# A two-layer encoder trunk: its opening rewritten, three projections first and memory's units behind

## The chip, the cores and the metric

One core of a Trainium2 chip runs the whole kernel as one program. The engines are TensorE (PE, with its weight loads as PEld), VectorE (DVE), ScalarE (ACT), GpSimd (POOL) and SyncE (SP, which here only issues DMAs). Each engine works through its own list of instructions in a fixed order; semaphores make one wait for another. The metric is the device time in microseconds (us) of one execution, less is better.

## The reference, cut to what matters

Batch 1, 1024 tokens, width 1024, two layers (A, then B). All tensors are float32.

```
mem_n = rmsnorm(mem, norm_mem)                       # 256 memory tokens
for i in range(2):
    h = rmsnorm(x, norm_mix[i])                      # x * rsqrt(mean(x^2)) * gain
    mk, mv = split(mem_n @ w_mem_kv[i])              # 4 heads of 64 each
    q, k, v, qm = split(h @ w_in[i])                 # A: 12 q, 4 k, 4 v heads; B: 12 of each; 4 qm heads
    y_tok = windowed_gqa(q, k, v, sink)              # i = 0; neighbourhood_attn for i = 1
    y_mem = softmax(qm mk^T / 8) mv
    x = x + concat(y_tok, y_mem) @ w_out[i]
    h = rmsnorm(x, norm_ffn[i])
    x = x + (silu(h @ w_gate) * (h @ w_up)) @ w_down[i]
out = rmsnorm(x, norm_final)
```

The norm of a token is one factor r = rsqrt(mean(x^2) + eps) for all its features. So (x * gain * r) @ W is the same as ((x * gain) @ W) * r: the factor can be multiplied in before the projection or behind it.

## The kernel before, in words

Tokens lie along the free dimension, in two halves of 512; features lie on the 128 partitions, in eight blocks k = 0..7. A weight is kept as units of 128 output columns: a tile of 128 x 1024, eight blocks of 128 x 128.

Every product is done in three passes. An operand is split into a high part (a cast to fp32r, on ACT, `hi`, L106) and a low part (operand minus high part, on DVE or POOL, `lo`, L109). `steps` (from L133) issues for each k three matmuls: high by high, high by low, low by high. A unit on one half is 24 matmuls of 512 columns; a unit on the 256 memory tokens is 24 of 256 columns.

The opening is everything ahead of layer A's attention:

- Memory's units: eight (four of each layer) of `w_mem` times `mhl`, the memory tokens times their gain, without the norm's factor. `finish_wm` multiplies the factor in when it reads a sum, and splits the keys (units 0 and 1 of a layer) or transposes and splits the values (units 2 and 3).
- `norms[0]`, the norm of the first half of x: squares on ACT, added up on DVE (`Norm.merge`), summed over partitions by four small matmuls into `st`; DVE adds eps (`nv`), POOL takes the power -0.5 (`nr`), DVE makes a diagonal matrix (`diag`), and a matmul with ones spreads it over all partitions (`bc`). `Norm.split` multiplies x by gain and `bc` and splits the result into `hT`, the operand of the projections.
- `first_dense` then runs three projections of the first half (units 0, 10 and 8 of `w_in_a`: a q and k unit, a memory-query unit, a v unit; their tiles are called wf), and beside them the norm and split of the second half. The sums stay in PSUM.
- `first_units` (in the layer's loop) reads these three sums (`put`), runs the same three units on the second half, transposes v (`vtr`), and fetches the next units (wqq, wqk, ...). From there on the attention's heads run, with the other projections pulled in between; the first scores `S` are those of a memory head, with keys mKH, mKL, which are read back from a buffer in HBM.

Order of work: the program text gives a priority, and a scheduler of the framework that runs at build time lays down the list of each engine, so that the lists don't follow the text in all places. Tiles come from pools with a fixed number of buffers; whoever takes a buffer waits for its last reader. The names in the rows: wm is a memory unit's weight, wf one of the first three units', mm the PSUM tile of a unit's sum, sq a square, mt a memory sum in SBUF, mvT its transpose.

Of the kernel before, what the change touches and what calls it, by code (L numbers as in the profile page):

```python
# [41 lines left out]
def trunk_kernel(ctx: ExitStack, tc: tile.TileContext, a: dict, out: bass.AP):  # L42
# [110 lines left out]
    def first_dense(layer, norm, more=iter(()), split=()):  # L153

        pre = []
        src = a["w_in_a"] if layer == 0 else a["w_in_b"]
        todo = (norm.add(x[k][1]) for k in range(len(norm.xs), NK))
        parts = norm.split(layer, hT[1], 6 if layer else 4)
        for n, u in enumerate(FIRST[layer]):
            w = split[n] if n < len(split) else load_w(src[u], eng=None if layer == 0 else nc.gpsimd, name="wf")  # L160
            if layer:
                wide[:] = True, (4, 2, 3)[n]
            ps = mm_tile()
            for i, _ in enumerate(steps(ps, w, hT[0])):
                next(more, None)
                if layer == 0 and len(norm.xs) < NK:
                    if n or i > 1:
                        run_some(todo, 2)
                elif next(todo, 0) is not None and (n or i > 3):
                    next(parts, None)  # L170
            if n == 1:
                run(more)
            pre.append((w, ps))
        run(parts)
        return pre
# [15 lines left out]
    class Norm:  # L191


        def __init__(self, n=HS, summed=NK):
            self.n, self.acc, self.xs, self.st, self.dg = n, [], {}, None, None
            self.summed = summed
# [90 lines left out]

    with tc.tile_pool(name="mp", bufs=1, reuse_waits="tile") as mp:
        phase[:] = mp, 8, 5
        memt = mp.tile([P, NK, NM], F32, name="memt")  # L290
        warm = mp.tile([P, P], F32, name="warm")
# [3 lines left out]

        def load_wm(i):
            ws[i] = raw_tile("wm")
            nc.sync.dma_start(ws[i], a["w_mem"][i // 4, i % 4])

        def split_wm(i, cs=slice(0, D)):  # L300
            if i not in whl:
                whl[i] = wp.tile([P, 2, D], F32R, tag="whl", name="wm", bufs=3)
            w = whl[i]
            hi(w[:, 0, cs], ws[i][:, cs])
            lo(w[:, 1, cs], ws[i][:, cs], w[:, 0, cs])

        def load_x(f, k):
            t = mp.tile([P, 2, HS], F32, tag=f"x{k}{f}", name=f"x0_{k}{f}")
            nc.sync.dma_start(
                t, a["x"][k : k + 2].rearrange("m p t -> p m t")[:, :, f * HS : (f + 1) * HS]  # L310
            )
            x[k][f], x[k + 1][f] = t[:, 0], t[:, 1]

        ws, whl = {}, {}
        ws[0] = raw_tile("wm0")
        nc.sync.dma_start(memt[:, :2], a["mem"][:, :2])
        nc.scalar.dma_start(ws[0][:, :HS], a["w_mem"][0, 0][:, :HS])
        nc.sync.dma_start(gains, a["gains"])
        nc.sync.dma_start(memt[:, 2:4], a["mem"][:, 2:4])
        nc.scalar.dma_start(ws[0][:, HS:], a["w_mem"][0, 0][:, HS:])  # L320
        nc.sync.dma_start(memt[:, 4:], a["mem"][:, 4:])
        load_wm(1)
        load_x(0, 0)
        load_x(0, 2)
        load_x(0, 4)
        load_x(0, 6)
        load_wm(2)
        nc.sync.dma_start(ident, a["ident"])
        load_wm(3)
        nc.sync.dma_start(sink, a["sink"].to_broadcast([P, NH]))  # L330
        split_wm(0, cs=slice(0, HS))


        mh = []
        mhl = mp.tile([P, NK, 2, NM], F32R, name="mhl")
        mem_norm = Norm(NM)
        for k in range(NK):
            t, g = mhl[:, k], gains[:, 4, k : k + 1]
            nc.scalar.activation(t[:, 0], memt[:, k], AF.Copy, scale=g)
            nc.vector.scalar_tensor_tensor(  # L340
                t[:, 1], memt[:, k], g, t[:, 0].bitcast(F32), op0=ALU.mult, op1=ALU.subtract
            )
            mh.append(t)
            if k == 1:
                split_wm(0, cs=slice(HS, D))
        split_wm(1)
        hT = [[None] * NK, [None] * NK]
        norms = [Norm(), Norm()]
        for k in range(NK):
            norms[0].add(x[k][0])  # L350
        scale = mp.tile([P, NM], F32, name="mscale")
        kept, sums = [], {}

        def finish_wm(i):

            (kh, kl, vm), u, ps = kept[i // 4], i % 4, sums.pop(i)
            t = temp("mt", NM)
            if u < 2:
                nc.vector.tensor_tensor(t, ps[:, :NM], scale, op=ALU.mult)
                hi(kh[:, u], t)  # L360
                lo(kl[:, u], t, kh[:, u])
                return
# [13 lines left out]
        parts, early = iter(()), []  # L376
        for i in range(8):
            if i % 4 == 0:
# [4 lines left out]
                kept.append((kh, kl, vm))  # L383
            if i + 4 < 8:
                load_wm(i + 4)
                load_x(1, 2 * i)
            if i + 2 < 8:
                split_wm(i + 2)
            sums[i] = dense(whl[i], mh, NM)
            if i == 1:  # L390
                for _ in range(2):
                    nc.tensor.matmul(
                        ps_o.tile([P, HS], F32, tag="O", name="warm"), ones, x[6][0], start=True, stop=True
                    )
                norms[0].sums()
                for k in range(NK):
                    mem_norm.add(memt[:, k])
            if i == 2:
                parts = norms[0].split(0, hT[0])
                run_some(parts, 1)  # L400
                mem_norm.sums()
                nc.vector.tensor_scalar(nsink, sink, -1.0, None, op0=ALU.mult)
            if i == 3:
                nc.scalar.copy(scale, mem_norm.scale(ps_t))
                finish_wm(0)
            if i > 3:
                finish_wm(i - 3)
            if i > 2:
                run_some(parts, 2)
            if i > 5:  # L410
                early.append(load_w(a["w_in_a"][FIRST[0][i - 6]], name="wf"))

        def last_units():
            for i in (5, 6, 7):
                yield
                yield
                yield
                finish_wm(i)

        pre = first_dense(0, norms[1], last_units(), early)  # L420
        for l, (kh, kl, vm) in enumerate(kept):
            nc.sync.dma_start(memk_d[l, 0], kh.rearrange("p m k -> p (m k)").bitcast(F32))
            nc.sync.dma_start(memk_d[l, 1], kl.rearrange("p m k -> p (m k)").bitcast(F32))
            nc.sync.dma_start(memv_d[l], vm.rearrange("p b m i d -> p (b m i d)").bitcast(F32))

    for layer in range(2):
        is_a = layer == 0
        with tc.tile_pool(name=f"ap{layer}", bufs=1, reuse_waits="tile") as ap:
# [59 lines left out]
            class Unit:  # L488
# [371 lines left out]

        with (
# [725 lines left out]
```

## Time and profile before

| what | value |
|---|---|
| median of 3 runs | 2135.73 us (2135.31 to 2136.31) |
| profiled execution, first to last instruction (span) | 2130.8 us |
| lies around the span | 4.9 us (the median less the span) |
| PE busy | 2097.1 us, 98% |
| DVE, ACT, POOL busy | 1517.2 us (71%), 1065.8 us (50%), 576.8 us (27%) |

Sections 1 and 2 of the profile's page give the busy share of each engine over the whole span and in 40 slices; the first slice and a half (53 us a slice) hold the opening. PE's digit is 8 in the first slice and 9 in all the others but the last. The chain that ended last is 90% PE. How to read the rows further down: the timeline gives start, length, engine, line, operation and tiles of instructions that follow one another on an engine (xN: N of them merged), and in brackets how long the engine stood idle before them and whom it waited for.

### The profile page before, as it was taken

Reading aid. Unit: us, or ns where it says so; the run is one execution under the profiler, and the core shown is the slowest. Engines: PE = TensorE matmul, PEld = TensorE weight load, DVE = VectorE, ACT = ScalarE, POOL = GpSimd, SP = SyncE. Lnnn points to the kernel's source line nnn. Section 1 sums busy time; section 2 is a strip of 40 time slices with the busy share of each in tenths; the row PEclk is TensorE's granted clock in tenths of the full one; section 3 lists DMA queues with packets and bytes.
Section 4 is the critical chain, followed back from the end, with each engine's and each line's share of the span. In section 5 each row is a group of like instructions: output and inputs, shape, how many; then the busy total and the mean of one; then the engine's idle time right before and its main releaser. Section 6 shows DMA issues by size and latency. Waiting matters only on the chain.

```text
span 2130.8 us, 29089 instructions
## 1 busy us (share of the span) xinstructions
PE 2097.1 (98%) x10320; PEld 1752.8 (82%) x10320; DVE 1517.2 (71%) x2481; ACT 1065.8 (50%) x2046; POOL 576.8 (27%) x618
## 2 busy tenths in 40 slices
PE   8999999999999999999999999999999999999998
PEld 7788888878888888888778888888888888888887
DVE  7677787788666666867766666667976666677676
ACT  6577775443434334344465666654443434344442
POOL 0343330233443430000233223203243443410000
PEclk9999999999999999999999999999999999999999
DMA  6321028323323327866232222275233323267662
GB/s 247 114 92 44 31 68 295 112 90 123 109 90 111 105 106 252 307 210 210 70 92 82 73 62 68 87 254 165 64 113 112 109 95 114 100 246 258 199 226 89
DMA packets 121042, 287.29 MB, mean 135 GB/s; under 512 B 12224, under 2 KB 20672, under 8 KB 120896
## 3 DMA queue, kind: packets, MB, share of 16 engines
q1 hardware_dynamic: 113584, 272.71, 38.1%
q10 hardware_dynamic: 7312, 12.72, 1.6%
q8 instruction: 82, 1.34, 0.3%
q14 instruction: 64, 0.52, 0.1%
HBM read 210.40 MB, written 68.94 MB: 131 GB/s over the span
## 4 chain that ended last, share of the span: by engine, by line
PE 90%; DVE 3%; ACT 3%; DMA 1%; issue 1%; POOL 1%; SPq 0%; DVEq 0%; ACTq 0%; POOLq 0%
PE X L952 17%; PE Y L952 16%; PE mm L139 16%; PE X L1383 11%; PE Y L1383 8%; PE po L139 8%; PE S L619 3%; PE O L682 3%; PE pT L662 3%; PE X L1034 2%; PE Y L1034 2%; DMA wd_kept<-in_w_dn 1%; POOL wS L909 0%; DMA x<-in_x 0%; PE bc L255 0%
## 5 line engine op out<-in xcount | busy, mean ns | idle before, releaser
L952 PE MATMUL Y<-hB,wgu 128*128 128x512 f32 x1056 | 255.5, 391 | 0.8 <-ACT c L972 0.8
L952 PE MATMUL X<-hB,wgu 128*128 128x512 f32 x1056 | 254.8, 391 | 0.0
L1383 PE MATMUL X<-hB,wd 128*128 128x512 f32 (+1 forms) x1092 | 243.8, 383 | 1.0 <-DVE x L1347 1.0
L109 DVE TENSOR_TENSOR wgu<-wS,wgu 128x1024 fp32r<-128x1024 f32 (+1 forms) x124 | 152.9, 1233 | 121.8 <-ACT wgu L106 121.5
L1383 PEld LDWEIGHTS X<-hB,wd 128*128 128x128 f32 x1092 | 200.1, 188 | 42.0 <-issue 2.4
L952 PEld LDWEIGHTS Y<-hB,wgu 128*128 128x128 f32 x1056 | 196.7, 188 | 43.4 <-ACT c L972 1.7
L952 PEld LDWEIGHTS X<-hB,wgu 128*128 128x128 f32 x1056 | 195.9, 188 | 39.9
L647 POOL TENSOR_SCALAR p<-p,stat 128x384 f32<-128x384 f32 (+1 forms) x256 | 139.7, 565 | 310.8 <-DVE stat L644 207.5
L139 PE MATMUL mm<-hT,wqk 128*128 128x512 f32 x672 | 196.1, 405 | 1.5 <-DVE KL L109 1.5
L106 ACT CAST wgu<-wS 128x1024 fp32r<-128x1024 f32 (+1 forms) x124 | 114.3, 923 | 149.6 <-POOL wS L909 124.6
L139 PE MATMUL po<-yT,wo 128*128 128x512 f32 x768 | 184.8, 394 | 0.0
L1383 PE MATMUL Y<-hB,wd 128*128 128x512 f32 x792 | 180.7, 389 | 0.1
L1383 PEld LDWEIGHTS Y<-hB,wd 128*128 128x128 f32 x792 | 148.5, 188 | 31.6 <-ACT hB L106 0.5
L240 POOL TENSOR_TENSOR nr<-nv,neg_half 128x4 f32<-128x4 f32 (+1 forms) x12 | 11.3, 938 | 600.5 <-DVE nv L239 600.5
L139 PEld LDWEIGHTS po<-yT,wo 128*128 128x128 f32 x768 | 142.8, 188 | 29.7 <-issue 1.0
L952 PE MATMUL X<-hT,wgu 128*128 128x512 f32 x624 | 150.2, 391 | 0.0
L106 ACT CAST hB<-b_raw 128x512 fp32r<-128x512 f32 x154 | 89.5, 618 | 110.6 <-DMA b_raw<-b_d 95.0
L909 POOL TENSOR_TENSOR wS<-wgu_raw 128x512 f32<-128x512 f32 x44 | 61.1, 1388 | 294.8 <-DVE wgu L109 294.8
L952 PEld LDWEIGHTS X<-hT,wgu 128*128 128x128 f32 x624 | 116.8, 188 | 26.3
L634 ACT ACTIVATE p<-p,stat 128x256 f32<-128x256 f32 (+1 forms) x192 | 112.4, 587 | 51.5 <-DVE stat L630 49.2
L109 DVE TENSOR_TENSOR pl<-pT,ph 128x384 fp32r<-128x384 f32 (+1 forms) x256 | 118.0, 493 | 19.4 <-ACT ph L106 16.5
L952 PE MATMUL Y<-hT,wgu 128*128 128x512 f32 x528 | 129.9, 390 | 0.0
(185 smaller groups left out, 4201.5 us busy)
## 6 DMA issues: line engine op xcount, KB each, us to landing
wgu_raw<-in_w_gu SPq DMA_DIRECT2D x92, 512.0 KB
wd_raw<-in_w_dn SPq DMA_DIRECT2D x70, 512.0 KB
b_raw<-b_d SPq DMA_DIRECT2D x70, 512.0 KB
b_d<-c SPq DMA_DIRECT2D x88, 256.0 KB
b_d<-t SPq DMA_DIRECT2D x66, 256.0 KB
wo_raw<-in_w_out SPq DMA_DIRECT2D x32, 512.0 KB
xr_d<-x ACTq DMA_DIRECT2D x32, 256.0 KB
xr<-xr_d SPq DMA_DIRECT2D x16, 512.0 KB
```

Source lines behind the costliest of these rows:

```text
L106: nc.scalar.copy(dst, src)
L109: (eng or nc.vector).tensor_tensor(dst, src, h.bitcast(F32), op=ALU.subtract)
L139: nc.tensor.matmul(ps[:, :n], l, r, start=start and i == 0 and j == 0, stop=stop and i == len(order) - 1 and j == 2,)
L619: nc.tensor.matmul(s_[:, :n], Q[self.h][:, qb * P : (qb + 1) * P], k, start=j == 0, stop=j == 1)
L634: nc.scalar.activation(p[:, :n], p[:, :n], AF.Exp, bias=m1, scale=-1.0, accum_out=s1)
L647: nc.gpsimd.tensor_scalar(p[:, :n], p[:, :n], ri[:, i : i + 1], 1.0, op0=ALU.mult, op1=ALU.mult)
L662: nc.tensor.transpose(tr[:, j * P : (j + 1) * P], p[:, j * P : (j + 1) * P], ident)
L682: nc.tensor.matmul(o[:, c0 : c0 + w * P], self.value(j), t[:, s0 : s0 + w].rearrange("p j q -> p (j q)"), start=j == js[0] and t is self.p ...
L909: sub = lambda o, p_, q_: nc.gpsimd.tensor_tensor(o, p_, q_, op=ALU.subtract)
L952: nc.tensor.matmul(ps, l, r, start=n in (0, 1, 3, 6) and k == 0 and i == 0, stop=k == 3 and i == 2, skip_group_check=True,)
L1034: nc.tensor.matmul(bank[:, at : at + h2], l, r, start=start and k == 0 and i == 0, stop=stop and k == 1 and i == 2, skip_group_check=True,)
L1383: nc.tensor.matmul(bank[:, c], l, r, start=i in (0, 1, 3, 6) and p == 0 and n == 0, stop=p == HF - 1 and n == 2, skip_group_check=True,)
```

## The change

The opening is written anew; layer B's `first_dense` stays as it was, and behind the opening only one thing is added.

1. The three projections of the first half run first, on tokens without the norm's factor: `unscaled` makes high and low part of x times gain straight from the loaded x. Their weights and x are loaded first; memory's tokens and weights behind them.
2. The squares of the first half: four on POOL, four on ACT; they are added on POOL (three) and DVE (four). When the sum is there, the factor for every token goes into `unit_scale`, and the three sums are multiplied by it into SBUF tiles (`first_sums`).
3. Memory's units come behind, values first (`mem_order`), on a pool tag of their own. The low parts of units 0, 1, 5 and 7 go to POOL, those of 2, 3, 4 and 6 stay on DVE. The squares of the second half are added on POOL (`adder`). Its split follows beside units 4 to 7.
4. Because `hT` of the first half has no factor now, each later unit of layer A multiplies its first-half sum by `unit_scale` into a tile `u` before `put` reads it (nine units).

The core of the diff:

```diff
+            self.summed, self.adder = summed, adder or nc.vector
...
-            nc.vector.tensor_tensor(one, one, sq, op=ALU.add)
+            self.adder.tensor_tensor(one, one, sq, op=ALU.add)
...
+        raws = [raw_tile("wf_raw") for _ in range(3)]
+        src = [a["w_in_a"][u] for u in FIRST[0]]
+        nc.scalar.dma_start(raws[0][:, :HS], src[0][:, :HS])
+        load_x(0, 0, each=True)
+        nc.scalar.dma_start(gains, a["gains"])
+        load_x(0, 2)
+        nc.scalar.dma_start(raws[0][:, HS:], src[0][:, HS:])
+        load_x(0, 4)
+        load_x(0, 6)
+        for n in (1, 2):
+            nc.sync.dma_start(raws[n], src[n])
...
+        norms = [Norm(), Norm(adder=nc.gpsimd)]
...
+        def unscaled(k):
+            g = gains[:, 0, k : k + 1]
+            t = hp.tile([P, 2, HS], F32R, tag="h", name="hT")
+            nc.scalar.activation(t[:, 0], x[k][0], AF.Copy, scale=g)
+            nc.vector.scalar_tensor_tensor(
+                t[:, 1], x[k][0], g, t[:, 0].bitcast(F32), op0=ALU.mult, op1=ALU.subtract
+            )
+            hT[0][k] = t
...
+        split_raw(wf[0], raws[0], cs=slice(0, HS))
+        for k in range(4):
+            unscaled(k)
+            square(k, nc.gpsimd)
...
+        for k in range(1, 4):
+            join(0, k, nc.gpsimd)
+        sums = [mm_tile() for _ in range(3)]
+        run(steps(sums[0], wf[0], hT[0]))
...
+        split_wm(0, nc.gpsimd)
+        run(steps(sums[1], wf[1], hT[0]))
+        last = steps(sums[2], wf[2], hT[0])
+        run_some(last, 4)
+        norms[0].acc = [squares[0]]
+        norms[0].sums()
...
+        run(last)
+        split_wm(1, nc.gpsimd)
+        nc.scalar.copy(unit_scale, norms[0].scale())
+        for n in range(3):
+            nc.vector.tensor_tensor(first_sums[n], sums[n], unit_scale, op=ALU.mult)
...
             if i + 2 < 8:
-                split_wm(i + 2)
+                load_wm(i + 2)
+                split_wm(i + 2, nc.gpsimd if i in (3, 5) else None)
...
+            if i < 3:
+                for k in range(3 * i, min(3 * i + 3, NK)):
+                    norms[1].add(x[k][1])
...
+            if i == 3:
+                norms[1].sums()
...
+                    if is_a and f == 0:
+                        t = ap.tile([P, HS], F32, tag="u", bufs=2, name="u")
+                        nc.vector.tensor_tensor(t, ps, unit_scale, op=ALU.mult)
+                        ps = t
```

POOL's list from its first work to the first weights of the attention; before:

```order
L240 TENSOR_TENSOR nr<-nv,neg_half 128x4
L240 TENSOR_TENSOR nr<-nv,neg_half 128x2
L240 TENSOR_TENSOR nr<-nv,neg_half 128x4
L568 TENSOR_SCALAR bias<-dist 128x384 x2
L109 TENSOR_TENSOR wqq<-wqq_raw,wqq 128x256 x4
```

and now (nr with 4 columns is a norm of x, with 2 columns memory's; wm in four pieces of 256 is the low part of one memory unit's weight):

```order
L362 TENSOR_TENSOR sq<-x_00_138 128x512 x2
L362 TENSOR_TENSOR sq<-x_20_142 128x512 x2
L365 TENSOR_TENSOR sq<-sq 128x512 x3
L109 TENSOR_TENSOR wm<-wm 128x256 x8
L233 TENSOR_TENSOR nr<-nv,neg_half 128x4
L233 TENSOR_TENSOR nr<-nv,neg_half 128x2
L219 TENSOR_TENSOR sq<-sq 128x512 x7
L109 TENSOR_TENSOR wm<-wm 128x256 x4
L233 TENSOR_TENSOR nr<-nv,neg_half 128x4
L109 TENSOR_TENSOR wm<-wm 128x256 x4
L625 TENSOR_SCALAR bias<-dist 128x384 x2
L109 TENSOR_TENSOR wqq<-wqq_raw,wqq 128x256 x4
```

Before, POOL only took the powers; now the first power stands behind two weights, and the second half's seven additions stand behind the power of memory's norm.

PE's list in the middle of memory's units, now (st is the partition sum of a norm: 4 matmuls of one column for x, 2 for memory; bc spreads the factor):

```order
L139 MATMUL mm<-hT,wf 128x512 x12
L248 MATMUL bc<-diag,ones 128x512
L139 MATMUL mm<-mhl,wm 128x256 x24
L212 MATMUL st<-inv_d,sq 128x1 x2
L139 MATMUL mm<-mhl,wm 128x256 x48
L248 MATMUL bc<-diag,ones 128x256
L139 MATMUL mm<-mhl,wm 128x256 x16
L430 MATMUL mvT<-ident,mt 128x128 x2
L139 MATMUL mm<-mhl,wm 128x256 x8
L212 MATMUL st<-inv_d,sq 128x1 x4
L139 MATMUL mm<-mhl,wm 128x256 x14
```

The last `st` there, of the second half, stands between memory's units 3 and 4; before, it stood behind all eight, among the projections.

ACT's list where the attention begins; before:

```order
L516 COPY vT<-mm 128x16x32
L626 ACTIVATE p,stat<-S,stat 128x256
L106 CAST wqq<-wqq_raw 128x1024
L106 CAST V<-vtr 128x4x64 x2
L626 ACTIVATE p,stat<-S,stat 128x256
```

and now:

```order
L515 ACTIVATE QS<-mm 64x512
L569 COPY vT<-mm 128x16x32
L106 CAST V<-vtr 128x4x64 x4
L683 ACTIVATE p,stat<-S,stat 128x256 x3
L106 CAST wqq<-wqq_raw 128x1024
```

The cast of wqq stood behind one exponential and now stands behind four casts of V and three exponentials; on PE all the scores of the first half-head and one more stand ahead of wqq's matmuls now.

## Rows read from the trace of the kernel before

**Rows 1.** Busy by stretch: us, PE, PEld, DVE, ACT, POOL, granted clock, DMA share, GB/s.

```profile
0.00:81.00 81.00, 71.98 (x382) 60.36 (x383) 60.94 (x107) 47.56 (x88) 5.46 (x9) 0.98 0.61 217
81.00:2130.80 2049.80, 2025.16 (x9939) 1692.42 (x9937) 1456.27 (x2374) 1018.25 (x1958) 571.38 (x609) 1.00 0.39 132
81.00:330.00 249.00, 243.70 (x1377) 204.42 (x1376) 187.08 (x494) 189.59 (x507) 98.84 (x174) 1.00 0.22 71
```

**Rows 2.** Who PE waited for in the first 110 us: total, times, longest.

```profile
PE mm L139 <- DVE wf L109: 2.5, 1, 2.5
PE bc L255 <- DVE diag L243: 1.8, 1, 1.8
```

**Rows 3.** Busy by stretch, PE alone, at 29 us: us, PE, granted clock, DMA, GB/s.

```profile
29.00:32.00 3.00, 2.83 (x11) 0.50 0.71 277
```

**Rows 4.** Chain of work that ended last, from 55 us: start, length, what.

```profile
59.58 21.59 PE mm L139 x95
...
89.86 0.48 PE S L619 x4
```

**Rows 5.** Timeline of ACT: start, length, what, idle before it.

```profile
8.12 1.71 ACT L339 ACTIVATE mhl<-memt,gains 128x256 fp32r<-128x256 f32 x4 [0.47 <-DMA memt<-in_mem]
...
13.54 1.16 ACT L203 ACTIVATE sq<-x 128x512 f32<-128x512 f32 x2 [0.20 <-DMA x<-in_x]
14.88 1.15 ACT L203 ACTIVATE sq<-x 128x512 f32<-128x512 f32 x2 [0.19 <-DMA x<-in_x]
...
25.15 1.99 ACT L106 CAST wm<-wm 128x1024 fp32r<-128x1024 f32 x2
...
81.20 0.59 ACT L516 COPY vT<-mm 128x512 f32<-128x512 f32 x1 [1.70 <-PE mm L139]
81.96 0.48 ACT L626 ACTIVATE p<-S,stat 128x256 f32<-128x256 f32 x1 [0.17 <-DVE stat L625]
...
82.42 1.04 ACT L106 CAST wqq<-wqq_raw 128x1024 fp32r<-128x1024 f32 x1
83.36 0.65 ACT L106 CAST V<-vtr 128x256 fp32r<-128x256 f32 x2
```

**Rows 6.** POOL's instructions by form: line, tiles, count, busy us, mean ns, idle before.

```profile
L109 POOL TENSOR_TENSOR wf<-wf_raw,wf 128x256 fp32r<-128x256 f32 x12 | 13.6, 1164 | 14.1 <-ACT wf L106 14.1
L109 POOL TENSOR_TENSOR wqq<-wqq_raw,wqq 128x256 fp32r<-128x256 f32 x16 | 11.3, 744 | 17.1 <-ACT wqq L106 17.1
L240 POOL TENSOR_TENSOR nr<-nv,neg_half 128x4 f32<-128x4 f32 x9 | 9.2, 1018 | 569.0 <-DVE nv L239 569.0
```

**Rows 7.** Timeline of DVE: start, length, what, idle before it.

```profile
21.84 2.10 DVE L226 TENSOR_TENSOR sq<-sq 128x256 f32<-128x256 f32 x6
...
61.60 1.89 DVE L109 TENSOR_TENSOR hT<-h,hT 128x512 fp32r<-128x512 f32 x3
...
81.44 0.76 DVE L625 TENSOR_REDUCE stat<-S 128x1 f32<-128x256 f32 x2 [1.21 <-PE S L619]
```

**Rows 8.** POOL at L909, 128x512, two inputs: ns min/median/max, first and last start.

```profile
L909 POOL TENSOR_TENSOR wS<-wS,wgu_raw x44: 1287/1358/1628, 373.1 to 1853.9; 128x512 f32<-128x512 f32 x44
L909 POOL TENSOR_TENSOR wS<-wgu_raw x44: 1292/1297/1806, 395.7 to 1879.4; 128x512 f32<-128x512 f32 x44
L909 POOL TENSOR_TENSOR wS<-wgu_raw,wS x44: 1286/1736/2274, 397.3 to 1880.7; 128x512 f32<-128x512 f32 x44
```

**Rows 9.** Timeline of PE: start, length, what.

```profile
18.54 3.09 PE L139 MATMUL mm<-mhl,wm 128*128 128x256 f32 x24
...
38.30 0.44 PE L366 MATMUL mvT<-ident,mt 128*128 128x128 f32 x2
...
55.37 0.95 PE L219 MATMUL st<-inv_d,sq 128*128 128x1 f32 x8
...
83.51 1.79 PE L139 MATMUL mm<-hT,wqq 128*128 128x512 f32 x5 [0.34 <-ACT wqq L106]
```

**Rows 10.** Timeline of DVE in layer B's opening, where POOL splits weights beside it.

```profile
1039.44 4.13 DVE L226 TENSOR_TENSOR sq<-sq 128x512 f32<-128x512 f32 x4
```

More of the change, by code (lines that the diff above doesn't have):

```diff
@@ L285, in trunk_kernel @@
     x = [[None, None] for _ in range(NK)]
+    around = ExitStack()
+    ep = around.enter_context(tc.tile_pool(name="ep", bufs=1, reuse_waits="tile"))
+    unit_scale = ep.tile([P, HS], F32, name="unit_scale")
+    first_sums = [ep.tile([P, HS], F32, name=f"first{n}") for n in range(3)]
     with tc.tile_pool(name="mp", bufs=1, reuse_waits="tile") as mp:
@@ L307, in load_x @@
[L307 to L311, printed above, removed]
-            x[k][f], x[k + 1][f] = t[:, 0], t[:, 1]
[L314 to L318, printed above, removed]
@@ new lines, in split_wm, with load_x @@
+        def split_wm(i, eng=None):
+            whl[i] = mp.tile([P, 2, D], F32R, tag="wmhl", name="wm", bufs=3)
+            split_raw(whl[i], ws[i], eng)
+        def load_x(f, k, each=False):
+            t = mp.tile([P, 2, HS], F32, tag="x0", name=f"x0_{k}{f}", bufs=6)
+            cols = slice(f * HS, (f + 1) * HS)
+            if each:
+                for m in range(2):
+                    nc.sync.dma_start(t[:, m], a["x"][k + m][:, cols])
+            else:
+                nc.sync.dma_start(t, a["x"][k : k + 2].rearrange("m p t -> p m t")[:, :, cols])
+            x[k][f], x[k + 1][f] = t[:, 0], t[:, 1]
@@ new lines, in trunk_kernel @@
+        wf = [wp.tile([P, 2, D], F32R, tag="whl", name="wf", bufs=3) for _ in range(3)]
+        hT = [[None] * NK, [None] * NK]
+        norms = [Norm(), Norm(adder=nc.gpsimd)]
+        mem_norm = Norm(NM)
+        squares = {}
+        def unscaled(k):
[6 more added lines that the diff above has]
+            hT[0][k] = t
@@ L374, in finish_wm @@
                 )
-        parts, early = iter(()), []
+            if u == 3:
+                nc.sync.dma_start(memv_d[l], vm.rearrange("p b m i d -> p (b m i d)").bitcast(F32))
+        parts = iter(())
         for i in range(8):
@@ L382, in trunk_kernel @@
                 vm = mp.tile([P, 2, NMH, 2, HD], F32R, name=f"mv{l}", tag="mv", bufs=2)
[L383 to L386, printed above, removed]
+                kept[l] = kh, kl, vm
             if i + 2 < 8:
-                split_wm(i + 2)
+                load_wm(i + 2)
+                split_wm(i + 2, nc.gpsimd if i in (3, 5) else None)
+            if i < 2:
+                load_x(1, 4 + 2 * i)
             sums[i] = dense(whl[i], mh, NM)
[L390 to L395, printed above, removed]
+            if i == 0:
@@ L403, in trunk_kernel @@
             if i == 3:
-                nc.scalar.copy(scale, mem_norm.scale(ps_t))
-                finish_wm(0)
+                norms[1].sums()
+            if i == 4:
+                parts = norms[1].split(0, hT[1])
+            if i > 1:
+                finish_wm(i - 2)
             if i > 3:
-                finish_wm(i - 3)
-            if i > 2:
                 run_some(parts, 2)
[L410 to L424, printed above, removed]
+        finish_wm(6)
+        run(parts)
+        finish_wm(7)
+        pre = list(zip(wf, first_sums))
     for layer in range(2):
@@ L858, in trunk_kernel @@
                 split_y(f, last_pair, ys[last_pair][:, f * HS : (f + 1) * HS])
+        if is_a:
+            around.close()
         with (
```

98 lines of the change are left out of this document (52 added, 46 removed).

## The prediction

> **What bounds the kernel now.** I read the busy times by stretch first [rows 1]. From 81 us to the end PE is busy 2025.2 of 2049.8 us; up to 81 us it is busy 72.0 of 81. The change works on the first stretch, and behind it adds only small products on DVE, so the question is when PE gets through the opening, and in what state the attention takes over. PE's waits of the first 110 us [rows 2] name two stretches where it stands still: 1.8 us for `diag` (the norm) and 2.5 us for a weight's low part. The 9.0 us without work hold these, the start, and the wait for loads. A part of the busy time is no work either: from 29 to 32 us the granted clock is 0.50, which is 1.2 GHz, behind the stall at `diag` [rows 3]. The chain [rows 4] then shows 95 matmuls of 512 columns in one piece from 59.58 to 81.17, 0.227 us each; that end, the end of the v unit, is what I compare. I call it T: 81.2 before. ACT's copy vT starts on it at 81.20 [rows 5].
>
> All of PE's work stays: three units on each half (144 matmuls) and eight of memory's. Two matmuls that only keep PE busy go, in a stretch where PE waits anyway.
>
> **The loads.** Before, x's first half was the last of 4.2 MB ordered for it; its last two pairs landed at 13.5 and 14.9 us, 1.35 us for 512 KB [rows 5]. Now 2.6 MB are ahead, three transfers fewer: 14.9 - 3 x 1.35 = 10.8 us. The first two blocks of x come much earlier, so PE starts at about 6 us as before, on another unit, and is paced by x and by DVE. `gains` stands behind ACT's table load now; the third block of x comes later than that in any case. Memory's loads are behind but are not needed before 15 us. SP's queue is otherwise the same work.
>
> **The chain that I think ends last** is not PE's own. After the last x block ACT has 2 copies of 512 (1.2), then, with wf's second unit landed at 12.2: cast (1.0), 2 squares (1.15), cast (1.0), 2 squares (1.15), cast of memory's unit 0 (1.0), 8 copies of memory at 1.71/4 each (3.4), cast of unit 1 (1.0) [rows 5]. That ends at 12.2 + 9.7 = 21.9. POOL makes the low part of unit 1 in four pieces of 0.74, 3.0, and only then takes the first power, 1.0 [rows 6]: 25.9. `diag` is one DVE operation on 512 columns, 0.6 to 0.7 (three `hT` in 1.89, [rows 7]): 26.6. PE has run its three units by then (72 x 0.227 = 16.4 and some waits) and spreads the factor at once.
>
> DVE follows in its own order: seven additions of memory's squares at 2.10/6 (2.5), the low part of memory's unit 2 (two times 0.63, 1.2), the three products with `unit_scale` (1.9, counted like the `hT` subtractions, all of them 512 columns), then `nv` of memory's norm, 0.2: 32.4 us. POOL waits for this `nv`, because memory's power stands ahead of the second half's additions: 0.7 to 1.0, so 33.3. Then seven additions of 512 columns on POOL, an operation that the trace has only at another line [rows 8]. The form that works in place has a median of 1.36, the fastest 1.30, the one that meets DVE most often 1.74. So 9.1 to 12.2 us; I take the mean of the three medians, 1.47, 10.3 in all: 43.6 us.
>
> PE meanwhile: spread factor 27.1, units 0 to 2 at 3.1 at most [rows 9], counted 3.0, the small sums 0.5, a spread 0.6, unit 3 and a transpose 3.4: 40.6. There the `st` of the second half stands in PE's list and waits for POOL, 3.0 us. Behind it stand all other units of memory and the second half's projections. From 43.6 on: `st` 0.95, unit 4 and a transpose 3.4, spread 0.5 (two matmuls of 512), units 5 to 7 at 3.0 and two transposes at 0.44 [rows 9], 9.9, the 72 projections 16.4. That is 31.1, so T = 74.7. A stall of 3 us can bring the half clock, as 29 to 32 us shows; half the rate over 3 us costs 1.4, and I count half of that: T = 75.4, or 5.8 us earlier than before. The split of the second half begins at about 48 and needs 16 DVE operations of 0.63, with memory's readings in between (counted as eight more of the same): it ends near 63, the last block is wanted at 67, and so is covered.
>
> **What is lost at the handover.** Before, wqq's cast came right behind the first exponential, 1.2 us after vT began (82.42 to 81.20), and PE began on wqq at 83.5 [rows 5, 9]. The matmuls of wqq's first half and all the scores around them were through at 90.34 [rows 4], 9.1 us after vT. Now, counted from vT: copy 0.6, transposes to 1.7, four casts of V in two pairs of 0.65 [rows 5], DVE's four low parts behind them (0.38 each, at the rate of 0.76 for two, [rows 7]) to 3.1, two maxima of scores 0.76, two exponentials at the pitch of 0.46 (81.96 to 82.42) to 4.5, the third score, which needs the bank of the first, its maximum and exponential to 5.2, cast 1.0, first piece on POOL 0.74: PE goes on at 7.0. The rest of wqq is 22 matmuls, 5.0, and two scores 0.5: 12.5, with one pair of scores (0.24) more done than before. So 12.5 - 0.2 - 9.1 = 3.2 us lost. Behind it PE is busy 243.7 of 249 us [rows 1], so little of this is made up.
>
> **The products `u`.** Nine of 0.63 to 0.69 on DVE, which is busy 187 of 249 us there [rows 1]. Nothing, if they fit the gaps; 6.2 us, if each delays PE. They are put where a unit's first half is done and its second half follows on PE (5.4 us of cover); I count 0.6. If the cover is gone, `Q` is late and the scores wait.
>
> Sum: -5.8 + 3.2 + 0.6 = -2.0 us on a profiled span of 2130.8, hence about 2128.8 there. The runs' median lies 4.9 us above the span; 2135.73 - 2.0 = 2133.7.
>
> **A rule that speaks against it.** In layer B's opening POOL splits weights beside a DVE that adds squares. A POOL piece of 256 columns takes 1.16 us on the mean there and 0.74 elsewhere [rows 6], and four DVE additions of 512 take 4.13 us, 1.03 each instead of 0.63 [rows 7, 10]. So both are slowed when both read SBUF twice. The Trainium skill has a rule for it (SBUF — State Buffer, section "Who interferes with whom"): a DVE instruction with two inputs in SBUF and a GpSimd instruction that reads SBUF exclude each other, and the second stands until the first is done. By that rule the times would add up in full: the low parts of units 3 and 4 and a `diag` on DVE (1.2, 1.2 and 0.4) would lengthen POOL's seven additions from 9.1 to 11.9, 1.6 more than I count. The rows show that both sides lose; whether in full, they don't tell.
>
> **Rivals.**
> *POOL isn't last.* If its additions begin earlier or run at 1.30 without loss, or DVE's queue is shorter than I count, PE never stops at `st`: 3.0 and the 0.7 of clock are saved. -2.0 - 3.7 = -5.7, 2130.0 us. For it: DVE has gaps in my count, and 1.30 is the commonest time of one form [rows 8]. Against it: `nv` stands behind twelve other DVE operations since `diag`. 0.18.
> *The handover costs nothing*, because the three scores and exponentials overlap better than I string them together, or ACT has idle time behind: -2.0 - 3.2 = -5.2, 2130.5 us. Against it: the lists are fixed and each step waits for the one before. 0.10.
> *DVE and POOL slow each other throughout* (the slower side). DVE makes the low parts of x beside POOL's squares; at 1.03 instead of 0.63 ten operations cost 4 us on the way to the first `st`. The four pieces of unit 1 at 1.16 cost 1.7, the seven additions at 1.74 cost 1.9, and the handover falls to the half clock for 3 us, 1.5; if half of `u` shows too, 2.5 more. Half of the first item is hidden by the chain on ACT. -2.0 + 2 + 1.7 + 1.9 + 1.5 + 2.5 = +7.6, 2143.3 us. It becomes slower than before from about a fifth of these 9.6 us on, and slower by what can be told from two thirds. For it: the rows of layer B's opening. Against it: the products, maxima and spreads that read PSUM have one SBUF input, and DVE often waits in these stretches. 0.13.
> *The early start is no start*: PE still begins at 6 us and still waits for loads, so that the 5.8 don't come. Then +3.8, 2139.5. 0.04; the loads are moved by 4 us for certain.
>
> **Chances and range.** What is left, 0.55, is the forecast, with its own range 2131 to 2137 (T 2 us either way, the handover 1). A measurement of this kernel can tell about 0.2% from no change, 4.3 us: 2131.5 to 2140.0. Faster by more: nearly all of the first two rivals, 0.27, and 0.04 of the forecast's lower end, 0.31. Slower by more: two thirds of the third rival (0.09), half of the fourth (0.02) and 0.02 of the forecast's upper end, 0.13. Within: 0.56. The range 2128.0 to 2140.0 takes in the first two rivals to 2 us below their times and leaves out about 2 in 10.
>
> **What the profile after would show.** Right: PE's first matmuls have `wf`; `bc` of the first half at 27 us; an idle PE of some 3 us before the second half's `st` at 40 to 44, with POOL's `sq` as releaser; vT at 75 to 76; wqq's first matmul some 6 us behind vT, after a PE that waits for `stat` or wqq. Wrong: no wait at that `st` and vT before 73; or wqq within 3 us of vT; or seven POOL additions of over 1.7 each and vT near 80; or PE's idle time in the attention up by several us, with `u` as releaser.

## The result, and the profile after

The changed kernel takes 2140.33 us (median of 11 runs; 2135.73 before): ratio 1.0022, 95% interval 1.0013 to 1.0031. It is slower by 4.6 us, just more than the 4.3 us that the prediction counted as no change. The forecast was 2133.7; its range 2128.0 to 2140.0 misses the time by 0.3 us. One of the eleven executions took 4304.53 us and is left out of the ratio. The profiled execution has a span of 2137.5, 6.7 above that of before, and took 2139.33.

Busy time by stretch, after (columns as in [rows 1]):

```profile
0.00:81.00 81.00, 70.89 (x375) 60.11 (x376) 58.31 (x88) 46.29 (x85) 41.32 (x39) 0.94 0.54 194
...
81.00:330.00 249.00, 239.06 (x1349) 200.25 (x1347) 189.67 (x496) 186.49 (x501) 101.66 (x174) 0.99 0.21 67
```

Against [rows 1], up to 81 us PE is busy 1.1 us less, at a mean clock of 0.94 instead of 0.98, and from 81 to 330 us it is busy 4.6 us less. So in these two executions both the opening and the handover to the attention lost time (the last section shows how far two executions can be compared). POOL works 41.3 us in the opening instead of 5.5. Who PE waited for in the first 110 us, the answer to [rows 2]:

```profile
PE mm L139 <- DVE hT L352: 3.5, 3, 2.4
PE st L212 <- POOL sq L219: 3.4, 1, 3.4
PE S L676 <- ACT p L683: 2.9, 2, 2.2
...
PE pT L719 <- DVE pl L109: 1.1, 1, 1.1
```

The waits for a weight (2.5) and for `diag` (1.8) are gone, and others stand in their place. The timelines of DVE and POOL show where the wait for `hT` comes from. DVE (as [rows 7]; `hT` is now the low part of x, made straight from x):

```profile
6.27 4.72 DVE L352 SCALAR_TENSOR_TENSOR hT<-x,gains,hT 128x512 fp32r<-128x512 f32 x4 [0.28 <-ACT hT L351]
10.92 1.77 DVE L109 TENSOR_TENSOR wf<-wf_raw,wf 128x512 fp32r<-128x512 f32 x1
12.62 4.77 DVE L352 SCALAR_TENSOR_TENSOR hT<-x,gains,hT 128x512 fp32r<-128x512 f32 x4
...
30.68 0.69 DVE L236 TENSOR_TENSOR diag<-ident,nr 128x512 f32<-128x512 f32 x1 [1.14 <-POOL nr L233]
```

POOL (the additions at L219 answer to [rows 8], the weights to [rows 6]):

```profile
4.41 2.48 POOL L362 TENSOR_TENSOR sq<-x 128x512 f32<-128x512 f32 x2 [3.98 <-DMA x<-in_x]
7.51 2.95 POOL L362 TENSOR_TENSOR sq<-x 128x512 f32<-128x512 f32 x2 [0.61 <-DMA x<-in_x]
10.41 5.11 POOL L365 TENSOR_TENSOR sq<-sq 128x512 f32<-128x512 f32 x3
16.76 10.04 POOL L109 TENSOR_TENSOR wm<-wm 128x256 fp32r<-128x256 f32 x8 [1.24 <-ACT wm L106]
29.61 1.03 POOL L233 TENSOR_TENSOR nr<-nv,neg_half 128x4 f32<-128x4 f32 x1 [2.81 <-DVE nv L232]
...
38.51 10.00 POOL L219 TENSOR_TENSOR sq<-sq 128x512 f32<-128x512 f32 x7
```

Beside POOL's squares and additions one low part of 512 columns takes DVE 1.19 us, where `diag`, of the same size and with POOL idle, takes 0.69. A piece of a weight takes POOL 1.25 beside DVE and 0.74 in [rows 6]. PE (timeline, as [rows 9]) is paced by this:

```profile
14.43 0.98 PE L139 MATMUL mm<-hT,wf 128*128 128x512 f32 x3 [2.41 <-DVE hT L352]
16.12 11.87 PE L139 MATMUL mm<-hT,wf 128*128 128x512 f32 x44 [0.71 <-DVE hT L352]
...
31.52 1.10 PE L248 MATMUL bc<-diag,ones 128*128 128x512 f32 x2
...
48.56 1.87 PE L212 MATMUL st<-inv_d,sq 128*128 128x1 f32 x8 [3.37 <-POOL sq L219]
...
89.04 7.06 PE L139 MATMUL mm<-hT,wqq 128*128 128x512 f32 x24 [0.43 <-ACT wqq L106]
```

The first half's factor is spread at 31.5 instead of the 26.6 forecast, and `st` of the second half stands at 48.6 instead of 43.6. Behind the stall at this `st` and in the handover, from 85 us on, the granted clock is low (columns as in [rows 1], the clock third from the end; both stretches stood at 1.00 before). So it is from 15 to 20 us, behind the 2.4 us wait for `hT`: 0.68.

```profile
50.00:55.00 5.00, 5.00 (x27) 5.00 (x27) 2.76 (x6) 0.49 (x2) 2.22 (x3) 0.56 0.01 3
85.00:95.00 10.00, 7.42 (x26) 5.62 (x27) 2.61 (x8) 5.37 (x14) 5.93 (x10) 0.83 0.74 245
```

The chain of work that ended last now passes through POOL's additions; the projections of the second half stand in it in one piece, as in [rows 4], from 65.58 on:

```profile
44.68 2.49 POOL sq L219 x2
47.25 1.26 POOL sq L219
48.56 1.87 PE st L212 x8
...
65.58 16.44 PE mm L139 x72
```

ACT (timeline, as [rows 5]) gives T, the start of vT, and the place of wqq's cast:

```profile
82.05 0.58 ACT L569 COPY vT<-mm 128x512 f32<-128x512 f32 x1 [3.50 <-PE mm L139]
83.38 1.67 ACT L106 CAST V<-vtr 128x256 fp32r<-128x256 f32 x4 [0.75 <-PE vtr L532]
...
87.95 1.03 ACT L106 CAST wqq<-wqq_raw 128x1024 fp32r<-128x1024 f32 x1
```

T is 82.05, not 75.4.

### The profile page after: what moved, and what is told of

Read it like the earlier page. It is cut to its first block, busy times and chain, and to the rows that moved or that the text cites. A ratio compares the mean times of both kernels' runs of the same rounds, so it can differ in the third digit from the quotient of the medians.

```text
span 2137.5 us, 29102 instructions
## 1 busy us (share of the span) xinstructions
PE 2099.7 (98%) x10316; PEld 1754.1 (82%) x10316; DVE 1519.8 (71%) x2471; ACT 1065.2 (50%) x2043; POOL 614.8 (29%) x648
## 4 chain that ended last, share of the span: by engine, by line
PE 89%; DVE 4%; ACT 3%; issue 1%; POOL 1%; DMA 1%; SPq 0%; DVEq 0%; POOLq 0%; ACTq 0%
PE X L1011 17%; PE Y L1011 16%; PE mm L139 15%; PE X L1442 11%; PE Y L1442 8%; PE po L139 8%; PE S L676 3%; PE O L739 3%; PE pT L719 2%; PE X L1093 2%; PE Y L1093 2%; ACT p L691 1%; DVE pl L109 1%; PE st L212 0%; PE bc L248 0%
## 5 line engine op out<-in xcount | busy, mean ns | idle before, releaser
L109 DVE TENSOR_TENSOR hB<-b_raw,hB 128x512 fp32r<-128x512 f32 x154 | 99.8, 685 | 46.1 <-ACT hB L106 45.8
```

The lines of the kernel that those rows point to most:

```text
L109: (eng or nc.vector).tensor_tensor(dst, src, h.bitcast(F32), op=ALU.subtract)
```

## The experiments

Two marks in each trace tell the opening from the handover: T, and the first matmul of wqm, a weight that the attention reaches some 70 us later and that no variant touches. What lies between them is the handover with whatever of it is made up. (Medians of 5 to 11 runs; ratio to before on the same chip. T, wqm and span are those of one profiled execution each.) The rows of wqm, before and after, give the first and the last start in layer A:

```profile
L139 PE MATMUL mm<-hT,wqm x48: 390/396/478, 149.9 to 173.2; 128*128 128x512 f32 x48
L139 PE MATMUL mm<-hT,wqm x48: 389/396/478, 157.1 to 179.9; 128*128 128x512 f32 x48
```

| kernel | T | wqm - T | span | median | ratio, interval |
|---|---|---|---|---|---|
| before | 81.20 | 68.7 | 2130.8 | 2135.73 | |
| after | 82.05 | 75.0 | 2137.5 | 2140.33 | 1.0022 [1.0013, 1.0031] |
| e1 no POOL squares | 77.70 | 75.1 | 2132.6 | 2135.81 | 1.0003 [0.9995, 1.0012] |
| e2 and weights' low parts on DVE | 77.89 | 75.0 | 2133.2 | 2136.26 | 1.0005 [0.9996, 1.0014] |
| e3 next weight early | 83.81 | 73.0 | 2139.4 | 2140.38 | 1.0024 [1.0015, 1.0033] |
| e4 no `u` | 82.45 | 73.4 | 2137.1 | 2139.17 | 1.0020 [1.0012, 1.0029] |
| e5 additions on DVE | 76.16 | 75.4 | 2131.7 | 2134.98 | 0.9997 [0.9988, 1.0006] |
| e6 and squares on ACT | 74.90 | 75.1 | 2133.3 | 2134.57 | 0.9994 [0.9985, 1.0003] |
| e7 and next weight held back | 74.47 | 74.3 | 2130.3 | 2131.91 | 0.9981 [0.9972, 0.9989] |
| e8 after, next weight held back | 81.77 | 73.2 | 2135.7 | 2138.38 | 1.0014 [1.0006, 1.0023] |
| e9 e7, second wqq on DVE | 74.75 | 71.4 | 2129.6 | 2130.73 | 0.9977 [0.9967, 0.9987] |
| e10 e9, wqk on DVE | 74.42 | 70.0 | 2125.3 | 2128.20 | 0.9964 [0.9952, 0.9977] |
| e11 one input on POOL | 81.83 | 75.1 | 2139.2 | 2141.03 | 1.0029 [1.0019, 1.0040] |
| e12 before, three weights on DVE | 84.16 | 68.6 | 2135.5 | 2135.51 | 1.0000 [0.9991, 1.0009] |

**e1 and e2: POOL's share of the squares left out.** e1:

```diff
             unscaled(k)
-            square(k, nc.gpsimd)
...
-        for k in range(1, 4):
-            join(0, k, nc.gpsimd)
...
-        join(0, 4, nc.vector)
...
-        norms[0].acc = [squares[0]]
+        norms[0].acc = [squares[4]]
```

> The changed kernel without POOL's four squares and three additions of the first half (left out: blocks 0 to 3 are missing from that norm's sum). Theory L (DVE and POOL slow each other whenever both read two inputs from SBUF, and that is what made the opening late): DVE's eight hT subtractions, 1.19 us each in the changed kernel, fall to 0.6 to 0.7, the first weight's halves from 1.77 to 0.7; PE is through its three first units at about 27 instead of 31.5, and vT (82.05) comes at 77.5 to 78.5; the kernel is 3.5 to 4.5 us faster than the changed one, near 2136. Rival R (x's loads and PE's own list set the opening, DVE had slack): vT at 81 to 82, at most 1 us faster.

DVE, PE and POOL of e1 (timelines, one fence for each):

```profile
10.65 2.73 DVE L352 SCALAR_TENSOR_TENSOR hT<-x,gains,hT 128x512 fp32r<-128x512 f32 x4
```

```profile
6.22 16.36 PE L139 MATMUL mm<-hT,wf 128*128 128x512 f32 x60 [1.83 <-ACT hT L351]
...
26.79 1.10 PE L248 MATMUL bc<-diag,ones 128*128 128x512 f32 x2 [0.55 <-DVE diag L236]
...
43.84 1.50 PE L212 MATMUL st<-inv_d,sq 128*128 128x1 f32 x8 [3.37 <-POOL sq L219]
```

```profile
21.42 3.52 POOL L109 TENSOR_TENSOR wm<-wm 128x256 fp32r<-128x256 f32 x4 [0.38 <-ACT wm L106]
24.91 1.01 POOL L233 TENSOR_TENSOR nr<-nv,neg_half 128x4 f32<-128x4 f32 x1
```

A low part is back at 0.68 us, PE runs 60 matmuls in one piece, T is 4.35 earlier and the median 4.5 lower. (One DVE addition, which joins the two groups of squares, is gone as well.) And now the forecast's chain is there to 0.3 us: POOL's low part ends at 24.9, the factor is spread at 26.8, `st` begins at 43.8. Some of this is luck: ACT's cast of unit 1 ended at 21.3 instead of 21.9, and POOL's four pieces took 3.5 us instead of 3.0. In the changed kernel this chain was hidden behind a slower one: there POOL stood idle for 2.81 us ahead of the first power and waited for DVE's `nv`.

e2 also has `split_wm(0)` and `split_wm(1)` without POOL:

> As the one before, and the low parts of memory's units 0 and 1 on DVE instead of POOL, so that POOL has nothing but a power until the second half's additions. Theory L: DVE gets 2.4 us more of its own but loses none to POOL; memory's eight subtractions and the second wf at full rate; vT at 77 to 79, within 1 us of the one before. Rival R: DVE only has more to do, vT later than there by 2 us or more.

Within 0.5 us of e1. The factor comes 1.0 earlier (`bc` at 25.83), but the second half's additions wait for memory's norm as before, so PE only stands longer at `st`: 4.65 us instead of 3.37.

**e3: wqq loaded in mid-opening, into a buffer of its own.**

```diff
+    next_raw = ep.tile([P, D], F32, name="next_raw")
...
-            t = mp.tile([P, 2, HS], F32, tag="x0", name=f"x0_{k}{f}", bufs=6)
+            t = mp.tile([P, 2, HS], F32, tag="x0", name=f"x0_{k}{f}", bufs=5)
...
+                nc.sync.dma_start(next_raw, a["w_in_a"][1])
...
+                        raw = next_raw if is_a and self.at == 1 else None
```

> The changed kernel with the load of the first later unit's weight (wqq) issued in the middle of memory's units, into a tile of its own, instead of behind memory's stores; x's buffers in the opening are 5 instead of 6 for the room. Theory H (wqq's load stands late in SP's queue, so its cast was laid behind four casts of V and three exponentials, and PE runs dry at the handover): PE goes from vtr into wqq, vT stays at 82, wqq's first half and the scores around it are through 9 to 10 us behind vT instead of 14.4, and the kernel is 4 to 5 us faster than the changed one. Rival (the loss there is the half clock and the slow split of Q beside POOL's weights, which stay): at most 1.5 us faster.

No gain in the time. On ACT (timeline) the cast now stood ahead of the reading of the first sums, and waited for its own output buffer, which is free only when PE has used up a first weight:

```profile
76.60 1.05 ACT L106 CAST wqq<-next_raw 128x1024 fp32r<-128x1024 f32 x1 [5.68 <-PE mm L140]
77.55 0.61 ACT L106 CAST QS<-first 64x512 fp32r<-64x512 f32 x1
```

The reading of the first sums, which stood behind it, came 7 us later (77.55 instead of 70.15), and T 1.8 later (PE waited 1.8 us for vT there, 0.7 in the changed kernel). Between the marks the run won 2.0 us: PE took wqq 1.5 us behind T instead of 7.0. So at the handover the early weight helped, by less than the 4 to 5 us of the theory, and what it won there was lost ahead of T.

**e4: the nine `u` products left out** (the factor is missing in the first half of nine units).

```diff
-                    if is_a and f == 0:
-                        t = ap.tile([P, HS], F32, tag="u", bufs=2, name="u")
-                        nc.vector.tensor_tensor(t, ps, unit_scale, op=ALU.mult)
-                        ps = t
```

> The changed kernel without the nine products with the factor in the later units of layer A (left out: those projections lack the norm's factor). If these products cost PE time in the attention, 1 to 3 us faster than the changed kernel, most of it behind 96 us; if they lie beside other work, 0 to 0.6. vT at 82 either way.

1.2 us in the medians, 1.6 between the marks. Since the intervals of e4 and the changed kernel overlap, a gain isn't shown; what is shown is that the products cost nowhere near 6 us.

**e5 and e6: the stall at `st`, and both losses mended with nothing left out.** e5:

```diff
-        norms = [Norm(), Norm(adder=nc.gpsimd)]
+        norms = [Norm(), Norm()]
```

> The seven additions of the second half's squares go from POOL back to DVE; nothing else changes. Measures the stall of PE at the second half's st and the slow clock behind it, by themselves. Theory S (they are a loss of their own, carried to the end): POOL's additions took 10.0 us and ended at 48.5; on DVE they take 7 x 0.63 = 4.4 and end near 43, st no longer waits (3.4 us), the slow clock behind it goes (1.7 us): vT at 82.05 - 5.1 = 77 us, and the time is 4 to 5 us below the changed kernel's 2140.3, near 2135.8. Rival G (whatever the opening saves is waited for again at the handover to the attention): vT at 77, but wqq and the scores start no earlier than before, and the time stays within 1.5 us of 2140.3.

PE (timeline):

```profile
45.58 0.95 PE L212 MATMUL st<-inv_d,sq 128*128 128x1 f32 x8
```

5.4 us, a little above the expectation: `st` stands at 45.58 without a wait, the clock is 1.00 from 20 to 80 us, T is 5.9 earlier. e6 has this and:

```diff
-            square(k, nc.gpsimd)
...
-            join(0, k, nc.gpsimd)
...
-        join(0, 4, nc.vector)
+        for k in range(4):
+            square(k, nc.scalar)
+            join(4, k, nc.vector)
...
```

> As the run before, and the four squares of the first half that were on POOL go to ACT behind its other four; their additions go to DVE, so nothing is left out. Theory L+S (the lock of DVE and POOL while x is split, and the stall at st, are two losses and add up): PE's three units run in one piece from 6.2 us; the squares are later than when they were left out, by 4 x 0.575 us of ACT, so bc of the first half stands at 27 to 28 us; vT at 82.05 - 4.0 - 5.1 = 73 us; time 2140.3 - 4.0 - 4.5 = 2131.8, faster than the old kernel by about 4 us. Rival G: 2135 or more, since the run with the squares left out was already at 2135.8 and the handover eats the rest.

The two losses don't add up. T is 74.90, only 1.3 earlier than in e5 (73 was expected), and the median 0.4 lower. PE starts its units in one piece, but then waits 1.2 us at the first `bc`, 1.4 for a free sum and 1.0 at the second `bc`: DVE now has all additions and is itself late. 2134.57 is close to where the rival had put it (2135 or more).

**e7 and e8: wqq's load held back, its low part on DVE.** e7 is e6 with this, e8 the changed kernel with this (`next_raw` and the five buffers of x are as in e3; the `eng=` lines, here and below, are parts of one line):

```diff
...
         finish_wm(7)
+        nc.vector.tensor_copy(next_raw[:, :1], hT[1][7][:, 1, :1].bitcast(F32))
+        nc.sync.dma_start(next_raw, a["w_in_a"][1])
...
-eng=nc.gpsimd if is_a else None
+eng=nc.gpsimd if is_a and raw is None else None
```

> As the run before, and wqq, the first weight behind the opening, has a buffer of its own; its load is held back until the second half's split is done (one element of that split is copied into the buffer first), so that its cast stands in ACT's list behind the first sums and not ahead of them; its low part is made on DVE instead of POOL. Theory H (the handover's loss is the place of wqq's cast, behind three exponentials): PE takes wqq right behind vtr, the two waits for p (2.9 us) are filled with its matmuls, the attention's start is 4 to 5 us nearer to vT, and the time is 3 to 5 us below the run before, near 2128. Theory A (ACT and DVE are the bound at the handover, not the place of one cast): PE does wqq's matmuls earlier and waits as long for S, pT and u afterwards; within 1.5 us of the run before.

> The changed kernel with the early, held-back load of wqq and its low part on DVE alone; squares and additions stay on POOL. Theory H: vT stays at 82 us, PE goes on with wqq 1 us behind vtr instead of 5, 3 to 5 us below 2140.3, near 2136. Theory A: within 1.5 us of 2140.3, as in the run with the ungated early load.

e7 gains 2.7 us on e6 and e8 2.0 on the changed kernel: less than the place of the cast should give (3 to 5), more than the rival allows (1.5), though in e8 not by more than the noise. PE takes wqq 1.5 us behind T instead of 7.0, as expected. But then, in e7 (PE, then POOL):

```profile
89.80 0.38 PE L723 MATMUL pT<-ident,p 128*128 128x128 f32 x2
92.68 0.38 PE L723 MATMUL pT<-ident,p 128*128 128x128 f32 x1 [2.50 <-POOL p L708]
```

```profile
86.14 3.29 POOL L109 TENSOR_TENSOR wqk<-wqk_raw,wqk 128x256 fp32r<-128x256 f32 x4 [0.75 <-ACT wqk L106]
89.39 2.78 POOL L109 TENSOR_TENSOR wqq<-wqq_raw,wqq 128x256 fp32r<-128x256 f32 x4
92.14 1.84 POOL L708 TENSOR_SCALAR p<-p,stat 128x256 f32<-128x256 f32 x4
```

Half of what was won is waited for again some 14 us later: the scaled p stand on POOL behind two weights. e9 and e10 test this.

**e9 and e10: those weights' low parts on DVE** (e9 the second wqq, e10 wqk too). The edit is e10's, against e7; e9 has `(1, 3)`.

```diff
-eng=nc.gpsimd if is_a and raw is None else None
+eng=nc.gpsimd if is_a and self.at not in (1, 2, 3) else None
```

> As the run with the held-back load of wqq and ACT/DVE squares and additions, and the low part of the second wqq too is made on DVE (1.2 us) instead of on POOL (2.8 us). There, POOL took the weights of wqk and the second wqq from 86.1 to 92.1 and only then the four p, for which PE waited 2.5 us and fell to a clock of 0.78 for 5 us. Theory P (that wait is the queue on POOL): POOL takes p near 89.4, the wait for p falls below 0.5 us, the slow clock at 90 to 95 goes, and the time is 2 to 3 us lower, near 2129. Rival A (ACT and DVE bound): DVE's 1.2 us more hold back maxima and pl, pT waits for them instead; within 1 us of 2131.9.

> As the run before, with wqk's low part on DVE as well, so that POOL does nothing but p and the biases there. Theory P: no wait for p at all, but 1.2 us more on DVE, which stands ahead of QS; the same time as the run before to 1 us, near 2129. Rival A: 1 to 2 us slower than the run before.

The wait for p is gone in both, and the clock is 1.00 from 75 to 105 us. e9 gains 1.2 us (expected 2 to 3; the intervals of e7 and e9 overlap), e10 another 2.5 (expected none). POOL's p begin at 92.14, 90.98 and 89.76 in e7, e9 and e10. That DVE is the bound there isn't so: e10 gives it two more low parts than e7, 1.23 us each, and is 3.7 us faster. What e9 still has is a wait of 0.8 us for `pl`, and a split of Q of 1.17 us beside POOL's wqk; in e10 the wait is gone and the split takes 0.69. e10, at 2128.20, beats both kernels: 0.9964 [0.9952, 0.9977] against before.

**e11: POOL reads one tensor instead of two.** (It leaves out the squares of four of the first half's eight blocks.)

```diff
-                eng.tensor_tensor(squares[k], x[k][0], x[k][0], op=ALU.mult)
+                for _ in range(2):
+                    eng.tensor_scalar(squares[k], x[k][0], 1.0, 1.0, op0=ALU.mult, op1=ALU.mult)
...
-            join(0, k, nc.gpsimd)
+            for _ in range(2):
+                nc.gpsimd.tensor_scalar(squares[0], squares[0], 1.0, 1.0, op0=ALU.mult, op1=ALU.mult)
```

> The changed kernel with POOL's four squares and three additions replaced by fourteen multiplications of one tensor by a constant, in the same places (two for each); the squares of four of the first half's eight blocks are left out by that. From the biases (0.55 us for 384 columns) I estimate 0.74 us each, 10.3 us in all, like the 10.5 us before, so POOL is as busy and reads one tensor instead of two. Theory L1 (the loss on DVE hangs on POOL reading SBUF, however many tensors): the eight low parts of x take 1.0 to 1.2 us each as before, time 2139 to 2141. Theory L2 (it hangs on how much POOL reads at a time, two tensors): the eight take 0.7 to 0.8 each, PE's units start in one piece, vT 3 to 4.5 us earlier, time near 2136.5.

DVE, then POOL (timelines):

```profile
6.23 3.80 DVE L352 SCALAR_TENSOR_TENSOR hT<-x,gains,hT 128x512 fp32r<-128x512 f32 x4 [0.32 <-ACT hT L351]
...
10.97 4.14 DVE L352 SCALAR_TENSOR_TENSOR hT<-x,gains,hT 128x512 fp32r<-128x512 f32 x4
...
23.36 5.25 DVE L403 SCALAR_TENSOR_TENSOR mhl<-memt,gains,mhl 128x256 fp32r<-128x256 f32 x7
```

```profile
5.27 7.27 POOL L363 TENSOR_SCALAR sq<-x 128x512 f32<-128x512 f32 x7 [0.21 <-DMA x<-in_x]
12.51 7.21 POOL L377 TENSOR_SCALAR sq<-sq 128x512 f32<-128x512 f32 x6
19.69 7.84 POOL L109 TENSOR_TENSOR wm<-wm 128x256 fp32r<-128x256 f32 x8
28.75 1.03 POOL L233 TENSOR_TENSOR nr<-nv,neg_half 128x4 f32<-128x4 f32 x1 [1.23 <-DVE nv L232]
```

A low part takes 0.95 to 1.03 us: between the theories, nearer to the one that any reading by POOL costs DVE. My estimate of 0.74 for POOL was wrong (1.04 and 1.20), so the run is no equal load. It shows something else: PE's `st` of the first half came 3.3 us earlier than in the changed kernel (24.55 to 27.83), yet `diag` held PE up for 2.28 us, and T was the same to 0.2 us. POOL was done with the weights at 27.5, but it waited another 1.23 us for DVE's `nv`, which stands in DVE's list behind memory's low parts. Beside POOL's weights these took 0.75 us each (7 in 5.25); in e2, with POOL idle, 0.41 (8 in 3.25). So here too DVE, slowed beside POOL, ends last, at another place.

**e12: the old kernel with three weights' low parts on DVE.**

```diff
-eng=nc.gpsimd if is_a else None
+eng=nc.gpsimd if is_a and self.at not in (1, 2, 3) else None
```

> The old kernel, its opening untouched, with the low parts of the first three weights behind the opening (wqq, wqk, the second wqq) on DVE instead of POOL, as in the fastest variant so far (2128.2). It tells how much of that variant's 7.3 us is the new opening and how much this move by itself. Theory O (the gain is the opening's: vT at 74.4 instead of 81.2, 6.8 us): the old kernel gains at most 1.5 us by the move, near 2135. Rival M (the move alone does it, since POOL holds back p and slows DVE's splits in the old kernel too): 3 us or more, 2132 or less.

No difference (its T of 84.16 is taken up in the last section). So the 7.3 us of e10 aren't this move's alone. In the old kernel PE waits for POOL's p only 0.6 us in the first 330 us; in e7 it waits 2.5.

## Why the prediction was wrong

The sum in the profiled spans: T +0.85 instead of -5.8 (off by 6.65), and T to wqm +6.35 instead of +3.2 + 0.6 (off by 2.55). Behind the mark 0.5 us come back. That makes 8.7, the difference between -2.0 and +6.7. The split between the two marks is less sure than the sum: e12 runs the opening of before with T at 84.16, and against that T the new opening ends 2.1 us earlier, not 0.85 later. Against either it lacks most of the 5.8, and the 6.35 behind T is the same to 0.1 us with e12. In the medians the kernel lost 4.6, not 6.7, since the profiled execution of before was a lucky one (below); the offset of 4.9 us that I added was mostly that: an execution lies 1.8 us above its own span.

1. *The rate of DVE at the start: the step that failed.* I took PE "paced by x and by DVE" at 0.63 us for a low part, and let the chain on ACT and POOL end last. The low parts took 1.19 beside POOL's squares. That is the third rival's mechanism, to which I gave 0.13. I had halved its price on the ground that ACT's chain hid it. It didn't: without the squares (e1) `bc` moves from 31.5 to 26.8, where the chain was forecast, and the median by 4.5; the slow clock from 15 to 20 us goes with them (0.68 in the changed kernel, 1.00 in e1). The row that spoke for it [rows 10] was read, and then applied to the rival only, not to the forecast. The forecast's own chain held in e1, where it did end last, and its sizes were near: seven additions 10.0 us (10.3 forecast), the stall 3.4 (3.0), `st` at 43.8 (43.6).
2. *The slow clock: a term mis-sized.* I counted 0.7 us behind the stall at `st`. From `st` to T it takes 33.5 us in the changed kernel and 33.9 in e1; in e5, without a stall, 30.6, or 31.0 with the three matmuls that stand ahead of `st` there. So it cost 2.5 us in the changed kernel and 2.9 in e1; in e8 and e11, with 32.9 from `st` to T, it cost 1.9. The 2.5 with the stall of 3.4 is what e5 gave back in T. With item 1 (4.35 in T) the 1.8 us beyond the 0.7, and the stall's 0.4 beyond 3.0, make up nearly all of the 6.65.
3. *The handover.* PE's start on wqq was forecast at 7.0 us behind T and came at 6.99. What the forecast left out is the clock behind it, which only the third rival had, at 1.5: from 85 to 95 us it is 0.83, and the 24 matmuls took 7.06 instead of 5.5 us. The rest, some 1 us, is `u` and the split of Q behind it: the split took 2.29 us instead of 0.69 beside POOL's second wqq. `u` was counted at 0.6; e4 points to 1.2 to 1.6, within its noise.
4. *The second rival ("the handover costs nothing")* is excluded by the 6.35 us, and by e8 to e10, which win back 1.8 to 5.0 us between the marks. *The first ("POOL isn't last")* fails on the stall of 3.4 us at `st`, *the fourth* on its own terms: the loads came in time (ACT read the last block of x at 11 us without a wait for its load), and what was late was DVE. That its 2139.5 us lies nearest to the measured time is luck.

The Trainium skill has the rule (SBUF — State Buffer, section "Who interferes with whom") that a DVE instruction with two inputs in SBUF contends with a GpSimd instruction that reads SBUF, for a port pair that the section calls an exclusive lock. The traces agree with the pairing, for one input on GpSimd too (e11). They don't show that the times add up in full, as the prediction worked out from the rule. From 7.5 to 15.5 us POOL ran two squares and three additions, 6.8 us at 1.24 and 1.43 each, and DVE 6.4 operations (by their pitch), 4.1 us at 0.65; by this estimate 10.9 us of work went into 8.0.

What stays open: why e6 gained only 0.4 us on e5 in the medians while T moved by 1.3; and of e10's gain over e9, how much is the earlier p, how much the wait for `pl`, and how much the split of Q that POOL no longer disturbs.

## What to carry to other kernels

Work given to POOL because it "is idle" was paid by DVE here wherever DVE's own operations read two tensors in SBUF (0.68 us became 1.19): try it on ACT, or put it where DVE waits anyway. When a rival's row (two engines that slow each other) comes from another stage of the same kernel, use its rate in the forecast wherever the same two engines meet, not in the rival alone. And at a handover every list matters: a weight stood first behind three exponentials on ACT, then ahead of sums not yet there, and the next two stood in front of p on POOL; only when all of this was mended (e10) did the early end of the opening, 6.8 us in T, reach the end of the kernel in full, 7.3 us.

## What the runs showed that I had not expected

*One opening, two clocks.* e12 runs the opening of before unchanged, with the same waits, and has T at 84.16 instead of 81.20. Busy time by stretch in e12, and the same stretches before (PE's time and instructions come first, the granted clock stands third from the end; 0.51 is nearly all at 1.2 GHz, 1.00 is 2.4 GHz):

```profile
30.00:35.00 5.00, 5.00 (x24) 4.91 (x24) 3.94 (x8) 1.40 (x3) 0.00 (x0) 0.51 0.21 85
45.00:55.00 10.00, 7.50 (x26) 5.91 (x26) 9.80 (x17) 6.85 (x14) 0.00 (x0) 0.83 0.34 123
```

```profile
30.00:35.00 5.00, 5.00 (x35) 4.91 (x35) 3.91 (x8) 2.32 (x4) 0.00 (x0) 0.80 0.22 88
45.00:55.00 10.00, 8.66 (x39) 7.14 (x40) 10.00 (x18) 6.51 (x15) 0.00 (x0) 1.00 0.38 134
```

Behind the same two stalls the clock was low for longer in e12: 60 of memory's matmuls took 9.72 us instead of 8.44, and 28 projections 8.29 instead of 6.65, together 2.9. Why the clock rose later there isn't shown. The times of before, unchanged, lie between 2132.5 and 2139.1 us. An execution's time is 1.8 us above its span (2139.33 to 2137.5), so the profiled one of before took about 2132.6, 3.1 below the median. So T and the span of two single executions may differ by some 3 us with nothing changed ahead of T, and smaller differences are safe only in the medians. The way from T to wqm (68.7 and 68.6) and the lengths of the same stall (1.84 and 2.50 us in both) agreed.
